# Projecting two pairs of neighbourhood heads early, and their place taken by half-size gate products

## The chip, the cores and the metric

The kernel runs on one core of a Trainium2 chip. Its time is the device time of one execution in microseconds (us); the median of three runs is 2477.17 us (2473.93 to 2483.84). The engines are named as the profile names them: PE is the matrix engine (TensorE), PEld its weight load, DVE the VectorE, ACT the ScalarE, POOL the GpSimd engine, SP the SyncE, which here only issues DMAs.

## The reference

One encoder block over 512 tokens of width 2048, in fp32:

```
mod    = silu(c) @ w_ada + b_ada          -> sh1, sc1, g1, sh2, sc2, g2
h      = rms_norm(x) * (1 + sc1) + sh1
[qa,ka,va, qb,kb,vb, ga,gb] = h @ w_in    # 8 + 2 + 2 heads A, 3 x 8 heads B, two gates of 2048
ya     = global attention (8 query heads, 2 key heads, qk-norm, rotary)
yb     = neighbourhood attention (8 heads, windows of 8 x 16 tokens, bias)
x      = x + g1 * ((sigmoid(ga) * (ya @ w_oa) + sigmoid(gb) * (yb @ w_ob)) @ w_out)
h2     = rms_norm(x) * (1 + sc2) + sh2
x      = x + g2 * ((silu(h2 @ w_gate) * (h2 @ w_up)) @ w_down)
out    = rms_norm(x)
```

## The kernel before, in words

**fp32 by parts.** Every fp32 operand of a product is held as a high part and a low part (`split`: ACT copies the high part, rounded, DVE subtracts it from the source to get the low part). A product is three matmuls, high x high, high x low, low x high (`mm3`, lines 187 to 189 of the kernel before). Weights are loaded by SP into `raw` tiles of 512 KB and split into `whl` tiles.

**Two forms of projection.** `form1` projects 256 output columns: 16 blocks of k, two column blocks, three matmuls that move 512 columns each. `group7` projects 512 output columns by a Strassen-like scheme of seven half-size products: four steps `s`, seven products, 84 matmuls a step that move 256 columns each, 336 in all, where two `form1` would need 192 matmuls of 512 columns. `wforms` makes the sums of weight blocks that the seven products need in tiles `ta` and `tb` on DVE, and splits them. At the end of a group, seven DVE additions gather the seven banks into a tile `c`.

**The order of the stages** around the change: global attention (`att_a`), with the `form1` of the gates A 12 to 15 beside it and those of the gates B 0 to 3 behind it; then five `group7` (three of gates B, `gates7`, and two of the values of the neighbourhood heads, `values7`, kept in DRAM as `v_d`); then the neighbourhood attention, four pairs of heads (`hp`), each pair with its own `form1` for queries and keys and then `att_b` for two heads; then the product with `w_oa` (its gates come back from DRAM as `g`), `w_ob`, `w_out`, and the feed-forward part, which is made of `group7` throughout. Gates are kept in DRAM as `sg_a`, `sg_b`. Queries and keys of the neighbourhood heads aren't kept; `form1` leaves them in PSUM banks `mm`, and `queries` and `tokens_split` split them from there into `qh`, `ql`, `kh`, `kl`.

**One neighbourhood head** (`att_b`) is a chain over engines: scores on PE into two banks `S` (12 matmuls of 256 columns), bias on DVE (`sb`, the bias tile `bm` comes by DMA on ACT's queue), maximum on DVE (`mx`), exponential on ACT (`e`), reciprocal and scaling on DVE, transposes on PE into bank `T`, a split into `pth` on ACT and `ptl` on DVE, and products with the values on PE into bank `Y`.

**The modulation beside it.** The second half of `mod` is computed as 96 accumulations on DVE before the feed-forward part (`acc`, line 379): each takes one 512 KB tile `mw` of w_ada that POOL's queue loads (line 357). They are handed out by `advance(mods)`: `slot` counts up by `pace["rate"]` at each unit of weights or half head and takes a step when the count reaches 1. 64 of the tiles run from the neighbourhood attention to the end of the product with `w_oa`, where `finish` takes what is left; 32 more run until the end of `w_out`.

**Memory.** Pools on one side of SBUF are a stack. `p_o` holds the tiles of the five `group7` (`c`, `ta`, `tb`, a few `raw` and `whl`). It is released behind them, and `p_w` (the modulation's tiles) and `p_b` (queries, keys, values, biases of `att_b`) are put in its place; the first write to each waits until every reader and writer of `p_o` has ended, the DMA of `c` into `v_d` too.

**Who sets the order.** A scheduler orders each engine's instructions when the kernel is built, from the program's order and priorities. Each engine then takes its own in that order and waits on semaphores; an instruction that waits holds all behind it on its engine.

Of the kernel before, what the change touches and what calls it, by code (L numbers as in the profile page):

```python
# [112 lines left out]
def encoder_block(ctx: ExitStack, tc, xp, xT, c, ada1_w, ada2_w, b_ada, norm1_w, w_in, q_norm_w, k_norm_w, bias,  # L113
# [11 lines left out]
    io = tc.alloc_tile_pool(name="io", bufs=3, side="right")  # L125
    aside = tc.alloc_tile_pool(name="aside", bufs=2, side="right")
# [220 lines left out]
    mod = {"pool": None, "queue": nc.gpsimd, "next": 0, "end": 0, "accs": 2, "loads": 3}  # L347
# [5 lines left out]
    def fetch():  # L353
        while mod["pool"] and len(fetched) < mod["loads"] and mod["next"] < mod["end"]:
            n = mod["next"] + {2: 32, 3: 32, 4: -32, 5: -32}.get(mod["next"] // KT, 0)
            w = mod["pool"].tile([P, 1024], F32, tag="mw", name="mw", bufs=mod["loads"])
# [10 lines left out]
    def ada_acc(bias, done):  # L367

        acc = mod["pool"].tile([P, 1024], F32, tag="acc", name="acc", bufs=mod["accs"])
# [18 lines left out]
    def row_sum(acc, q, tag, dst, then=None):  # L388
        few = mod["loads"] == 1
        hl = [io.tile([P, 512], F32R, tag="io", name="acc" + t) if few else  # L390
              mod["pool"].tile([P, 512], F32R, tag="acc" + t, name="acc" + t, bufs=1) for t in "hl"]
        split(*hl, acc[:, q * 512:(q + 1) * 512], pin=behind)
        soon.append((1 if few else 2, lambda: row_products(hl, tag, dst, then)))

    def row_products(hl, tag, dst, then):
        y = bank(tag)
# [10 lines left out]
        soon.append((1 if mod["loads"] == 1 else 2, keep))  # L407

    def ada_mod(k0, to):
# [9 lines left out]
        def done(acc):  # L419
            soon.append((1, functools.partial(row_sum, acc, 0, "Y", halves[0])))  # L420
            soon.append((4, functools.partial(row_sum, acc, 1, "Y", halves[1], lambda: soon.append((1, columns)))))
# [3 lines left out]
    def ada_gate(col, dst, tags):  # L425
        return ada_acc(col, lambda acc: soon.extend((1 + q * (4 if mod["loads"] == 1 else 1),
                                                     functools.partial(row_sum, acc, q, tags[q], dst[q])) for q in range(2)))
# [247 lines left out]

    def wforms(w, k0, c0, turned=False, late=False):
# [5 lines left out]
        ta = wq.tile([P, 1024], F32, tag="ta", name="ta", bufs=2)  # L682
# [49 lines left out]
    def group7(wsrc, xs, order, dst, first_group=False, by_tokens=False):  # L732
# [3 lines left out]
        for n, s in enumerate(order):  # L736
# [147 lines left out]

    for h in range(4):
# [3 lines left out]
    gates(sg_a, GA, 12, 16)  # L889
# [29 lines left out]
    def feature_forms(s):  # L919
# [3 lines left out]
        sa = p_o[0].tile([P, 1024], F32, tag="ta", name="sa", bufs=2)  # L923
# [18 lines left out]
    gates(sg_b, GB, 0, 4)  # L942
    wq = p_o[0]
    more_buffers(1, 1)
# [5 lines left out]
    def gates7(n):  # L950
# [7 lines left out]
        group7(lambda s: wforms(w_in, 4 * s, GB + n * 512), hs, range(4), dst)  # L958
        S.activation(c[0], c[0], AF.Sigmoid)
        for f in range(4):  # L960
            nc.scalar.dma_start(sg_b[4 * n + f].rearrange("p (t n) -> p t n", t=2), quarters(c[0])[:, f // 2, :, f % 2])

    def values7(hh):
        v = result().rearrange("p (i n) -> p i n", i=NT)
        d = [[v[:, 2 * t:2 * t + 2, f * 256:(f + 1) * 256] for f in range(2)] for t in range(2)]
        group7(lambda s: wforms(w_in, 4 * s, VB + hh * 512), hs, range(4), lambda: d, by_tokens=True)
        nc.scalar.dma_start(v_d[hh], v)

    for n in range(1, 4):
        gates7(n)  # L970
# [4 lines left out]
    more_buffers(0, 0)  # L975

    p_w = tc.alloc_tile_pool(name="p_w", bufs=1, side="right")
    mod.update(pool=p_w, end=64)
    g1_d, g2_d = ([dram.tile([1, 512], F32, name=f"g{n}d{q}") for q in range(4)] for n in (1, 2))
    columns_of = lambda ks: (ada_mod(k, (s2, b_sc2, n2, t2, b_sh2)) for k in ks)  # L980
    gate_of = lambda c, dst, tags="YT": (ada_gate(c * D + q * 512, dst[q:], tags) for q in (0, 2))
    mods.extend(columns_of((0, 4)))
    mods.extend(gate_of(2, g1_d))
    mods.extend(columns_of((8, 12)))
    for half_gate in gate_of(5, g2_d, "TT"):
        mods.extend((half_gate, iter([None] * 4)))
# [50 lines left out]

    def queries(hi, lo, b):
        tokens_split(hi[:, 64:], lo[:, 64:], b)
        for t in (hi, lo):  # L1040
            S.activation(t[:, :64], t[:, T:], AF.Copy)
# [24 lines left out]
    later.extend([lambda: None] * 4 + [lambda: pace.update(rate=0.68)])  # L1066
    for hp in range(4):
        hh, h0 = hp // 2, 2 * hp
        qs, ks = [pair(p_b, "q", T + 64, 3) for _ in range(2)], [pair(p_b, "k", T, 3) for _ in range(2)]
        form1([w_in], QB + h0 * HD, 2, hT, [[bank("mm"), bank("mm")]], lambda w, j, b: queries(*qs[j], b))  # L1070
        form1([w_in], KB + h0 * HD, 2, hT, [[bank("mm"), bank("mm")]], lambda w, j, b: tokens_split(*ks[j], b))
        if hp % 2 == 0:
            v = [pair(p_b, "v", 512, NT) for _ in range(NT)]
            for i in range(0, NT, 2):
                vr = raw_tile("vr")
                nc.sync.dma_start(vr.rearrange("p (i n) -> p i n", i=2), v_d[hh][:, i:i + 2])
                for e in range(2):
                    split(*v[i + e], vr[:, e * 512:(e + 1) * 512])
# [31 lines left out]

# [542 lines left out]
```

## Time and profile before

| | |
|---|---|
| profiled execution, its own time | 2471.66 us |
| span of the profile | 2469.5 us |
| median of three runs, lowest, highest | 2477.17, 2473.93, 2483.84 us |
| PE busy | 2434.0 us, 99% of the span |
| DVE busy | 2011.8 us, 81% |
| ACT busy | 1076.2 us, 44% |
| mean DMA rate | 187 GB/s |
| chain that ended last | PE 80%, DVE 11%, DMA 3%, issue 3% |

The busy time of PE is modelled, so 99% doesn't say that PE runs at its best; the number of matmuls in a stretch says more. Where matmuls of 512 columns stand without a gap, 233 start in 50 us; where those of 256 columns do, 450. "Idle before, releaser" of a row names what ended the engine's wait.

### The profile page before, as it was taken

What the parts mean: (1) busy time and instruction counts of PE and PEld (TensorE: products, weight loads), DVE (VectorE), ACT (ScalarE), POOL (GpSimd) and SP (SyncE); (2) the same over time, 40 slices, a digit from 0 to 9 for tenths busy, and PEclk for the clock granted to TensorE, in tenths of its full rate; (3) what the DMA queues carried; (4) which work ended last, traced back from release to release, by engine and by line L of the source; (5) the groups of instructions that cost most, each with busy time, mean ns of one, the idle gap of its engine ahead of it and who ended that gap; (6) DMA issues with size and microseconds to landing.
All of it is one profiled execution on the core that took longest, in us unless ns stands there. A gap on an engine that the chain in (4) does not pass through costs nothing.

```text
span 2469.5 us, 42360 instructions
## 1 busy us (share of the span) xinstructions
PE 2434.0 (99%) x17327; PEld 2279.5 (92%) x17327; DVE 2011.8 (81%) x2704; ACT 1076.2 (44%) x1470; POOL 152.1 (6%) x257
## 2 busy tenths in 40 slices
PE   8999999999999999999999999999999999999998
PEld 7888888999888888888999999999999998999997
DVE  8995778987587768667899899898898886787877
ACT  5223545544344533237744444444444454434333
POOL 0100000000012111021000000000000000000010
PEclk9999999999999999999999999999999999999999
DMA  9864232444578687966444354444444456546563
GB/s 355 314 238 154 85 100 78 148 129 145 201 250 273 233 305 247 309 211 215 139 160 160 131 171 153 130 152 142 159 153 154 131 187 222 197 151 234 192 248 123
DMA packets 213730, 461.77 MB, mean 187 GB/s; under 512 B 15152, under 2 KB 59552, under 8 KB 204832
## 3 DMA queue, kind: packets, MB, share of 16 engines
q1 hardware_dynamic: 173872, 308.71, 37.6%
q0 software_dynamic: 30160, 133.77, 15.4%
q10 hardware_dynamic: 9504, 16.58, 1.8%
q8 instruction: 136, 2.23, 0.4%
q14 instruction: 58, 0.48, 0.1%
HBM read 412.84 MB, written 46.17 MB: 186 GB/s over the span
## 4 chain that ended last, share of the span: by engine, by line
PE 80%; DVE 11%; DMA 3%; issue 3%; ACT 1%; POOL 0%; DVEq 0%; SPq 0%; POOLq 0%; ACTq 0%
PE mm L189 16%; PE mm L187 16%; PE mm L188 16%; PE S L187 6%; PE S L189 6%; PE S L188 6%; PE Y L187 3%; PE Y L188 3%; PE Y L189 3%; DVE raw L516 2%; DVE whl L169 2%; DMA mw<-in_ada_w 2%; DMA raw<-in_w_down 1%; PE T L189 1%; PE T L188 1%
## 5 line engine op out<-in xcount | busy, mean ns | idle before, releaser
L167 ACT ACTIVATE whl<-raw 128x1024 fp32r<-128x1024 f32 (+1 forms) x483 | 454.3, 943 | 659.4 <-PE mm L189 273.9
L169 DVE TENSOR_TENSOR whl<-raw,whl 128x1024 fp32r<-128x1024 f32 (+1 forms) x483 | 519.6, 1088 | 133.0 <-ACT whl L167 128.7
L167 ACT ACTIVATE whl<-ta 128x1024 fp32r<-128x1024 f32 x124 | 131.3, 1059 | 179.3 <-PE mm L189 110.2
L167 ACT ACTIVATE whl<-tb 128x1024 fp32r<-128x1024 f32 x124 | 131.4, 1059 | 172.4 <-PE S L189 119.8
L169 DVE TENSOR_TENSOR whl<-ta,whl 128x1024 fp32r<-128x1024 f32 x124 | 151.5, 1222 | 54.1 <-ACT whl L167 53.5
L379 DVE SCALAR_TENSOR_TENSOR acc<-mw,cact,acc 128x1024 f32<-128x1024 f32 x124 | 159.4, 1287 | 19.2 <-DMA mw<-in_ada_w 18.9
L169 DVE TENSOR_TENSOR whl<-tb,whl 128x1024 fp32r<-128x1024 f32 x124 | 151.1, 1219 | 7.8 <-ACT whl L167 7.3
L357 POOL DMA_DIRECT2D mw<-in_ada_w x115 | 61.5, 535 | 1381.1 <-DVE acc L379 836.1
L687 DVE TENSOR_TENSOR ta<-raw,ta 128x512 f32<-128x512 f32 x124 | 85.4, 689 | 53.8 <-DMA raw<-in_w_down 24.9
L686 DVE TENSOR_TENSOR ta<-raw 128x512 f32<-128x512 f32 x124 | 85.4, 689 | 29.5 <-DMA raw<-in_w_down 27.0
L187 PE MATMUL mm<-x56h,whl 128*128 128x256 f32 x336 | 92.5, 275 | 0.0
L188 PE MATMUL mm<-x56l,whl 128*128 128x256 f32 x336 | 92.4, 275 | 0.0
L189 PE MATMUL mm<-x56h,whl 128*128 128x256 f32 x336 | 92.4, 275 | 0.0
L187 PE MATMUL mm<-whl,s 128*128 128x256 f32 x320 | 88.1, 275 | 0.0
L187 PE MATMUL mm<-x3h,whl 128*128 128x256 f32 x320 | 88.0, 275 | 0.0
L188 PE MATMUL mm<-x3l,whl 128*128 128x256 f32 x320 | 88.0, 275 | 0.0
L189 PE MATMUL mm<-x3h,whl 128*128 128x256 f32 x320 | 88.0, 275 | 0.0
L187 PE MATMUL S<-x56h,whl 128*128 128x256 f32 x320 | 88.0, 275 | 0.0
L188 PE MATMUL S<-x56l,whl 128*128 128x256 f32 x320 | 88.0, 275 | 0.0
L189 PE MATMUL S<-x56h,whl 128*128 128x256 f32 x320 | 88.0, 275 | 0.0
L188 PE MATMUL mm<-whl,s 128*128 128x256 f32 x320 | 88.0, 275 | 0.0
L189 PE MATMUL mm<-whl,s 128*128 128x256 f32 x320 | 88.0, 275 | 0.0
(1879 smaller groups left out, 8916.8 us busy)
## 6 DMA issues: line engine op xcount, KB each, us to landing
raw<-in_w_in SPq DMA_DIRECT2D x133, 512.0 KB, 4.3
mw<-in_ada_w POOLq DMA_DIRECT2D x115, 512.0 KB, 4.5
raw<-in_w_gate SPq DMA_DIRECT2D x92, 512.0 KB, 4.5
raw<-in_w_up SPq DMA_DIRECT2D x88, 512.0 KB, 4.5
raw<-in_w_down SPq DMA_DIRECT2D x88, 512.0 KB, 5.0
raw<-in_ada_w POOLq DMA_DIRECT2D x29, 1024.0 KB, 7.3
raw<-in_w_out SPq DMA_DIRECT2D x48, 512.0 KB, 4.8
ffd<-c SPq DMA_DIRECT2D x10, 1024.0 KB, 4.8
```

Of the source, the lines that this page charges most:

```text
L167: high = pin(S.activation(hi, src, AF.Copy))
L169: latest[:] = [high, pin(eng.tensor_sub(lo, src, hi))]
L187: nc.tensor.matmul(o, lh, rh, start=start, stop=False, **kw)
L188: nc.tensor.matmul(o, lh, rl, start=False, stop=False, **kw)
L189: nc.tensor.matmul(o, ll, rh, start=False, stop=stop, **kw)
L357: mod["queue"].dma_start(w, ada2_w[n * P:(n + 1) * P, :])
L379: behind(V.scalar_tensor_tensor(acc, part, cact[:, k:k + 1], acc, op0=ALU.mult, op1=ALU.add))
L516: V.scalar_tensor_tensor(raw, raw, 1.0, call, op0=ALU.mult, op1=ALU.mult, accum_out=y)
L686: V.tensor_sub(t1, b12, b11)
L687: V.tensor_sub(t2_, b22, t1)
```

## The change

Three things move together.

1. In place of the `form1` of gates A 12 to 15 beside the global attention stands a projection of queries and keys of heads 0 and 1 of the neighbourhood attention (`project(0)`); in place of the `form1` of gates B 0 to 3 stands that of heads 4 and 5 (`project(2)`). Both are evacuated by ACT and kept in DRAM (`qk_d`). Later, pairs 0 and 2 load them (`kept`) and split them from SBUF; pairs 1 and 3 are projected as before (`fresh`).
2. The gates that lost their place are made by `group7`: seven groups in place of five.
3. The modulation starts earlier: 18 of its tiles come in the seven groups, three accumulations a group (`by_steps`), from a pool `p_w0` for the accumulator and one `mw` buffer in `p_o`; 30 more tiles in the neighbourhood attention, and 48 from `w_oa` on in a pool `p_w2` that is now opened ahead of `w_oa`. The `finish` behind `w_oa` is gone. To make room, `ta` has one buffer in the groups where it had two, and `raw` four where it had five.

```diff
 def slot():
     pace["due"] = min(pace["due"] + pace["rate"], 1.5)
+    if mod["then"] and not fetched and mod["next"] == mod["end"]:
+        mod.update(mod["then"].pop())
...
-    ta = wq.tile([P, 1024], F32, tag="ta", name="ta", bufs=2)
+    ta = wq.tile([P, 1024], F32, tag="ta", name="ta", bufs=ta_bufs[0])
...
+                if r == ORDER[2] and 0 < n <= by_steps:
+                    advance(mods)
...
+def project(hp):
+    for n, base in enumerate((QB, KB)):
+        def evac(w, j, b):
+            o = aside.tile([P, T], F32, tag="go", name="qo")
+            S.activation(o.rearrange("p (h e i) -> p h e i", e=2, i=P), apart(b), AF.Copy)
+            nc.scalar.dma_start(qk_d[hp // 2][n][:, j], o)
+        form1([w_in], base + 2 * hp * HD, 2, hT, [[bank("mm"), bank("mm")]], evac)
...
-gates(sg_a, GA, 12, 16)
+project(0)
...
-gates(sg_b, GB, 0, 4)
+project(2)
...
-more_buffers(1, 1)
+more_buffers(0, 1)
...
-for n in range(1, 4):
-    gates7(n)
+mod.update(mw=p_o[0], end=18, few=True, delays=(0, 3, 0))
+for base, to, n in [(GA, sg_a, 3)] + [(GB, sg_b, n) for n in range(4)]:
+    gates7(base, to, n, 1)
 for hh in range(2):
     values7(hh)
...
-mod.update(pool=p_w, end=64)
+mod.update(mw=p_w, sums=[(p_w, 1), (p_w0, 1)], end=48, loads=3, few=False, bank="mm", delays=(1, 6, 3))
...
+def kept(hp, qs, ks):
+    for n, ts in enumerate((qs, ks)):
+        r = raw_tile("qkr")
+        nc.sync.dma_start(r.rearrange("p (j t) -> p j t", j=2), qk_d[hp // 2][n])
+        for j, (hi, lo) in enumerate(ts):
+            o = 0 if n else 64
+            split(hi[:, o:], lo[:, o:], r[:, j * T:(j + 1) * T])
+            if not n:
+                wrap(hi, lo)
...
 for hp in range(4):
...
-    form1([w_in], QB + h0 * HD, 2, hT, ..., lambda w, j, b: queries(*qs[j], b))
-    form1([w_in], KB + h0 * HD, 2, hT, ..., lambda w, j, b: tokens_split(*ks[j], b))
+    (fresh if hp % 2 else kept)(hp, qs, ks)
...
+mod["then"].append(dict(mw=p_w2, sums=[(p_w2, 2)], end=96))
-pace["rate"] = 0.45
+pace["rate"] = 0.42
 for j in range(0, KT, 2):
     form1([w_oa], ...)
-finish()
```

How the built order moves, at three places. First, PE behind the last `group7`. Before (`Y` is the bank of its last product, `mm<-h0h` the first query projection):

```order
L189 MATMUL Y<-whl,h15l 128x256
L187 MATMUL mm<-h0h,whl 128x512
L188 MATMUL mm<-h0l,whl 128x512
L189 MATMUL mm<-h0h,whl 128x512
L187 MATMUL mm<-h0h,whl 128x512
```

After:

```order
L190 MATMUL Y<-whl,h15l 128x256
L188 MATMUL S<-kh,qh 128x256 x2
L189 MATMUL S<-kl,qh 128x256
L190 MATMUL S<-kh,ql 128x256
L188 MATMUL S<-kh,qh 128x256
L189 MATMUL S<-kl,qh 128x256
```

Before, 193 matmuls of two projections follow the last `Y`; after, the 12 score matmuls of head 0 do, then three of the projection of pair 1, then the scores of head 1, then 16 more of that projection ahead of the first transposes.

Second, ACT at the same place, after (`vd` is the DMA of the last `c` to DRAM, `qkr` the kept queries and keys, `vr` the kept values):

```order
L989 DMA vd_4028<-c 128x2048
L168 ACTIVATE qh<-qkr 128x512 x2
L1066 ACTIVATE qh<-qh 128x64 x2
L1066 ACTIVATE ql<-ql 128x64
L168 ACTIVATE kh<-qkr 128x512
L1066 ACTIVATE ql<-ql 128x64
L168 ACTIVATE kh<-qkr 128x512
L168 ACTIVATE vh<-vr 128x512 x4
L1019 DMA bm<-in_bias 128x512 x2
L168 ACTIVATE whl<-raw 128x1024 x3
L1019 DMA bm<-in_bias 128x512
L1039 ACT_TABLE_LOAD
```

Before, the issue of the two biases stood directly behind the first weight split after `vd`, far ahead of the first scores. After, ten pieces of splits stand between, all of which write tiles of `p_b`.

Third, DVE behind the fresh keys of the second pair (heads 2 and 3), after:

```order
L170 TENSOR_TENSOR kl<-mm,kh 128x512 x2
L170 TENSOR_TENSOR kl<-qkr,kh 128x512
L1033 SCALAR_TENSOR_TENSOR sb<-S,bm 128x512 x2
L1035 TENSOR_REDUCE mx_7772<-sb 128x2
L1035 TENSOR_REDUCE mx_7802<-sb 128x2
L1036 TENSOR_SCALAR mx_7772<-mx_7772 128x2
L170 TENSOR_TENSOR ql<-qkr,qh 128x512
L1036 TENSOR_SCALAR mx_7802<-mx_7802 128x2
L170 TENSOR_TENSOR kl<-qkr,kh 128x512
L1042 RECIPROCAL rs_7774<-sm_7773 128x2
L1033 SCALAR_TENSOR_TENSOR sb<-S,bm 128x512
L1044 TENSOR_SCALAR e<-e,rs_7774 128x256 x2
```

Before, the heads of a pair stood beside the whole projection of the next pair. After, four heads (2 to 5) follow each other here, since pair 2 has no projection of its own, and share 79 of the 192 matmuls of pair 3's projection. From the first of these rows to the last `ptl` split of head 5, DVE has 66 rows.

More of the change, by code (lines that the diff above doesn't have):

```diff
@@ L345, in encoder_block, with sum_tile @@
     t2 = const.tile([P, KT], F32, name="t2")
-    mod = {"pool": None, "queue": nc.gpsimd, "next": 0, "end": 0, "accs": 2, "loads": 3}
+    mod = {"mw": None, "loads": 1, "sums": [(p_w0, 1)], "few": False, "bank": None, "then": [], "delays": (1, 6, 3), "queue": nc.gpsimd, "next": 0, "end": 0}
+    def sum_tile():
+        pool, bufs = mod["sums"][0]
+        mod["sums"].append(mod["sums"].pop(0))
+        return pool.tile([P, 1024], F32, tag="acc", name="acc", bufs=bufs)
     fetched = collections.deque()
@@ L353, in fetch @@
     def fetch():
-        while mod["pool"] and len(fetched) < mod["loads"] and mod["next"] < mod["end"]:
+        while len(fetched) < mod["loads"] and mod["next"] < mod["end"]:
             n = mod["next"] + {2: 32, 3: 32, 4: -32, 5: -32}.get(mod["next"] // KT, 0)
-            w = mod["pool"].tile([P, 1024], F32, tag="mw", name="mw", bufs=mod["loads"])
+            w = mod["mw"].tile([P, 1024], F32, tag="mw", name="mw", bufs=mod["loads"])
             mod["queue"].dma_start(w, ada2_w[n * P:(n + 1) * P, :])
@@ L367, in ada_acc @@
     def ada_acc(bias, done):
-        acc = mod["pool"].tile([P, 1024], F32, tag="acc", name="acc", bufs=mod["accs"])
+        acc = sum_tile()
         if bias is not None:
@@ L405, in keep, with ada_mod @@
                 then()
-        soon.append((1 if mod["loads"] == 1 else 2, keep))
-    def ada_mod(k0, to):
+        soon.append((2 if mod["delays"][2] > 1 else 1, keep))
+    def ada_mod(k0, to, tag):
         halves = [dram.tile([1, 512], F32, name=f"md{k0}{q}") for q in range(2)]
@@ L883, in att_a @@
         keep_y(h, yb)
+    qk_d = [[dram.tile([P, 2, T], F32, name=f"qk{hp}{n}") for n in range(2)] for hp in (0, 2)]
+    def project(hp):
[5 more added lines that the diff above has]
+            form1([w_in], base + 2 * hp * HD, 2, hT, [[bank("mm"), bank("mm")]], evac)
     for h in range(4):
@@ L975, in encoder_block @@
     more_buffers(0, 0)
+    ta_bufs[0] = 2
     p_w = tc.alloc_tile_pool(name="p_w", bufs=1, side="right")
[L978 to L986 removed]
+    mod.update(mw=p_w, sums=[(p_w, 1), (p_w0, 1)], end=48, loads=3, few=False, bank="mm", delays=(1, 6, 3))
     fetch()
@@ L1064, in attended, with kept_values, fresh @@
         split(*hl, yr)
-    later.extend([lambda: None] * 4 + [lambda: pace.update(rate=0.68)])
+    pace["rate"] = 0.65
+    def kept(hp, qs, ks):
[6 more added lines that the diff above has]
+                if not n:
+                    wrap(hi, lo)
+    def kept_values(hh):
+        v = [pair(p_b, "v", 512, NT) for _ in range(NT)]
+        for i in range(0, NT, 2):
+            vr = raw_tile("vr")
+            nc.sync.dma_start(vr.rearrange("p (i n) -> p i n", i=2), v_d[hh][:, i:i + 2])
+            for e in range(2):
+                split(*v[i + e], vr[:, e * 512:(e + 1) * 512])
+        return v
+    def fresh(hp, qs, ks):
+        form1([w_in], QB + 2 * hp * HD, 2, hT, [[bank("mm"), bank("mm")]], lambda w, j, b: queries(*qs[j], b))
+        form1([w_in], KB + 2 * hp * HD, 2, hT, [[bank("mm"), bank("mm")]], lambda w, j, b: tokens_split(*ks[j], b))
     for hp in range(4):
@@ L1069, in encoder_block @@
         qs, ks = [pair(p_b, "q", T + 64, 3) for _ in range(2)], [pair(p_b, "k", T, 3) for _ in range(2)]
-        form1([w_in], QB + h0 * HD, 2, hT, [[bank("mm"), bank("mm")]], lambda w, j, b: queries(*qs[j], b))
-        form1([w_in], KB + h0 * HD, 2, hT, [[bank("mm"), bank("mm")]], lambda w, j, b: tokens_split(*ks[j], b))
+        (fresh if hp % 2 else kept)(hp, qs, ks)
         if hp % 2 == 0:
[L1073 to L1078, printed above, removed]
+            v = kept_values(hh)
         if hp == 3:
@@ L1298, in first_pairs @@
         early[1] = ff_pair(0, 1, [c_p.tile([P, 1024], F32R, tag=t, name="e1", bufs=1) for t in ("mw", "acc")], nc.sync)
-    mod.update(pool=c_p, queue=nc.gpsimd, end=128, accs=1, loads=1)
+    mod.update(mw=c_p, sums=[(c_p, 1)], queue=nc.gpsimd, end=128, loads=1, few=True, delays=(1, 5, 1))
     for n in range(FU):
```

53 lines of the change are left out of this document (33 added, 20 removed).

## The prediction

> **What bounds the kernel now.** I read the page's busy times first, then the table of stretches, then the rows around the places that the change touches.
>
> ```profile
> span 2469.5 us, 42360 instructions
> PE 2434.0 (99%) x17327; PEld 2279.5 (92%) x17327; DVE 2011.8 (81%) x2704; ACT 1076.2 (44%) x1470; POOL 152.1 (6%) x257
> PE 80%; DVE 11%; DMA 3%; issue 3%; ACT 1%; POOL 0%; DVEq 0%; SPq 0%; POOLq 0%; ACTq 0%
> ```
>
> PE bounds the kernel, so a matmul saved counts where PE is dense, and a wait of PE counts everywhere. The stretches (us, then busy time and count of PE, PEld, DVE, ACT, POOL, the granted clock, the DMA share, GB/s) show where it is dense:
>
> ```profile
> 484.90:522.20 37.30, 37.30 (x337) 37.30 (x336) 31.15 (x40) 17.35 (x18) 0.00 (x0) 1.00 0.45 141
> 500.00:550.00 50.00, 50.00 (x450) 50.00 (x450) 40.69 (x50) 23.21 (x25) 0.00 (x0) 1.00 0.43 134
> 700.00:760.00 60.00, 59.59 (x303) 51.25 (x302) 48.84 (x68) 25.45 (x51) 11.30 (x21) 1.00 0.78 260
> 760.00:820.00 60.00, 59.67 (x301) 50.66 (x300) 46.06 (x65) 22.68 (x45) 12.24 (x22) 1.00 0.83 278
> 820.00:880.00 60.00, 53.28 (x254) 44.70 (x253) 47.55 (x72) 36.09 (x60) 9.41 (x16) 0.94 0.71 251
> 950.00:1000.00 50.00, 50.00 (x233) 43.79 (x232) 45.02 (x56) 17.38 (x22) 7.95 (x15) 1.00 0.81 278
> ```
>
> One `group7` takes 37.3 us, with 336 matmuls and DVE busy for 31. A matmul of 256 columns costs 50/450 = 0.111 us, one of 512 columns 50/233 = 0.2146. The neighbourhood attention (640 to 820) is dense too; PE loses 6.7 us, and some clock, only from 820 to 880, where heads 6 and 7 stand beside `w_oa`.
>
> **Part 1: the products.** The two `form1` beside the global attention and the two behind it stay in number: gates become queries and keys. Two more groups add 672 matmuls of 256 columns, 74.7 us; pairs 0 and 2 drop 384 of 512 columns, 82.4 us. On PE: **-7.7 us**. Dropped too are 16 weight splits, and 6 of 17 loads of ACT's function table; both lie beside PE, and I cost them at nothing. The new stores (eight of 256 KB on ACT's queue) replace eight stores of gates; the gates' new stores go out from `c` as those of the other groups do.
>
> **Part 2: the place behind the last group.** There the cover of PE is gone. Before:
>
> ```profile
> 626.78 0.28 PE L189 MATMUL Y<-whl,h15l 128*128 128x256 f32 x1
> 626.89 0.38 PE L187 MATMUL mm<-h0h,whl 128*128 128x512 f32 x1
> 628.99 0.69 DVE L773 TENSOR_TENSOR c<-c,Y 128x512 f32<-128x512 f32 x1
> 629.72 0.33 ACTq L967 DMA_DIRECT2D vd<-c  x1
> 633.90 0.82 ACTq L993 DMA_DIRECT2D bm<-in_bias  x2
> ...
> raw<-in_w_in SPq DMA_DIRECT2D x133, 512.0 KB, 4.3
> bm<-in_bias ACTq DMA_DIRECT2D x8, 256.0 KB, 3.7
> ```
>
> The first five rows are of the timeline (start, duration), the last two of the DMA issues (size, median us to landing). The last product of the groups ends at about E = 626.9, and PE goes on at once. The bias is the first write to `p_b`: it goes out 4.2 us after the store of `c`, when that has read its tile. All this was hidden by 41 us of projections. After, queries and keys wait for the same release and PE has nothing else: the scores stand first in its order, and the weights of pair 1 can't be there early, since the four `raw` buffers hold `qkr` and `vr`, which can't be split before `p_b` is free. The durations:
>
> ```profile
> L1007 DVE SCALAR_TENSOR_TENSOR sb<-S,bm 128x512 f32<-128x512 f32 x15 | 10.0, 682 | 1.1 <-PE S L189 1.1
> L1009 DVE TENSOR_REDUCE mx<-sb 128x2 f32<-128x512 f32 x15 | 9.9, 674 | 0.0
> L169 DVE TENSOR_TENSOR whl<-raw,whl 128x1024 fp32r<-128x1024 f32 x31 | 37.7, 1219 | 18.6 <-ACT whl L167 18.6
> L169 DVE TENSOR_TENSOR kl<-mm,kh 128x512 fp32r<-128x512 f32 x8 | 5.3, 690 | 6.4 <-ACT kh L167 6.4
> L167 ACT ACTIVATE qh<-mm 128x512 fp32r<-128x512 f32 x8 | 4.7, 587 | 8.0 <-PE mm L189 8.0
> L1041 ACT ACTIVATE ql<-ql 128x64 fp32r<-128x64 f32 x8 | 2.0, 253 | 8.6 <-DVE ql L169 8.6
> L167 ACT ACTIVATE vh<-vr 128x512 fp32r<-128x512 f32 x8 | 4.7, 622 | 6.0 <-DMA vr<-vd 6.0
> ```
>
> Back to back, each starts about 0.08 us before the recorded end of the last. From E: `c` complete +1.1 (in the after order no weight split stands between the seven additions, three stood there before), store read +5.3. ACT: two `qh`, two wraps, a wrap of `ql`, the first `kh` end at +7.3, and the first `kl` on DVE at +8.0: the scores of head 0 run from +8.0 to +9.3. The other splits keep ACT until about +10.1, and only then are the biases issued; they land 3.7 us later, +13.8. Two `sb` and two maxima (4 x 0.6) end at +16.2, then comes the first weight split, 1.2: PE gets its first projection matmul at +17.5. Idle: 17.5 less 1.3 of scores, 16.2 us. From then on 58 matmuls of 0.2146 and the heads' own cover DVE. The clock adds to it:
>
> ```profile
> 821.92 0.49 PE L187 MATMUL S<-kh,qh 128*128 128x256 f32 x2 [1.02 <-ACT kh L167]
> 823.31 0.38 PE L188 MATMUL S<-kl,qh 128*128 128x256 f32 x1 [0.89 <-DVE kl L169]
> 826.81 0.63 PE L188 MATMUL mm<-ya0l,whl 128*128 128x512 f32 x1
> 827.24 0.63 PE L189 MATMUL mm<-ya0h,whl 128*128 128x512 f32 x1
> 828.15 0.38 PE L187 MATMUL mm<-ya0h,whl 128*128 128x512 f32 x1
> ```
>
> After idle pieces of 1.0 and 0.9 us, matmuls of 512 columns start 0.43 us apart until 827.7: half speed for some 3.4 us, a loss of 1.7. So **+17.9 us**. Bounds: with the bias landing in 2.5 us and one step less of waiting, 14; with slower landings beside three loads of `mw`, 20.
>
> **Part 3: heads 2 to 5 in a row.** DVE from the keys of head 3 to the last split of head 5 has, for four heads, 8 each of `sb`, maximum, two small ones, two scalings, `ptl`; beside them 5 weight splits, 5 accumulations, 10 half splits (keys, queries, values, a sum). The rows not shown yet:
>
> ```profile
> L379 DVE SCALAR_TENSOR_TENSOR acc<-mw,cact,acc 128x1024 f32<-128x1024 f32 x42 | 53.8, 1281 | 14.8 <-DMA mw<-in_ada_w 14.5
> L169 DVE TENSOR_TENSOR ptl<-T,pth 128x512 fp32r<-128x512 f32 x12 | 8.3, 689 | 3.3 <-ACT pth L167 2.8
> L1018 DVE TENSOR_SCALAR e<-e,rs 128x256 f32<-128x256 f32 x26 | 7.9, 346 | 0.1
> L1010 DVE TENSOR_SCALAR mx<-mx 128x2 f32<-128x2 f32 x14 | 2.3, 161 | 0.0
> ```
>
> Less 0.08 each: 8 x (0.60 + 0.59 + 2 x 0.08 + 2 x 0.27 + 0.61) = 20.0; 5 x 1.14 + 5 x 1.20 + 10 x 0.61 = 17.8; together 37.8 us. PE has there 96 matmuls of 256 columns (10.7), 32 transposes (some 3, an estimate from 0.4 us for four) and 79 of the projection (17.0): 30.6. DVE bounds the stretch: with 0.8 ahead (the first `kh`) and 0.9 behind (the last products with the values) 39.5 us, +8.9. DVE also waits at its start for scores and exponentials; I take **+10**, between +6 (the chains overlap better) and +15 (DVE waits at each head). Before, 301 and 303 matmuls in 60 us show that these heads cost PE next to nothing.
>
> **Part 4: the modulation.** The groups get three accumulations each, 3 x 1.2, on DVE's 31 of 37.3 us: covered. At their start DVE was late before (first row, of the waits: us in all, times, longest):
>
> ```profile
> PE mm L189 <- DVE whl L169: 1.9, 2, 1.3
> ...
> 873.03 0.49 PE L398 MATMUL T<-acch,ones_r 128*128 128x512 f32 x1 [2.20 <-ACT acch L167]
> 875.29 0.59 PE L398 MATMUL T<-accl,ones_r 128*128 128x512 f32 x1 [1.76 <-DVE accl L169]
> 864.23 6.63 DMA yr<-y
> ```
>
> One accumulation and single `ta` there: **+1** (0 to 5). The stall at 873, 4 us and a half-speed phase of 1.7, came from the row sum behind an attention output that landed after 6.6 us, amid loads of `mw` (the last row, of the chain). After, 18 tiles are gone to the groups, and `w_oa` takes them at rate 0.42 without `finish`: I take **-5** of this 5.7 (0 to -10 with the smaller gaps from 840 on).
>
> **The sum:** -7.7 + 17.9 + 10 + 1 - 5 = +16.2, from the profiled execution's 2471.66 to **2488 us**. That execution lies 0.2% under the median, within the runs' spread.
>
> [...]
>
> **Rivals.**
> - *No change.* The relief of the DMA queues is full (-10), parts 2 and 3 take their low ends (14 and 6), part 4 none: -7.7 + 14 + 6 - 10 = +2.3, 2474 us. For it: 14.5 us of DVE's waits for `mw` in the rows above. Against: PE lost little of that.
> - *Faster*, by one mechanism: the projections of pairs 1 and 3 go on covering, so that parts 2 and 3 cost nothing: -7.7 + 1 - 5 = -11.7, 2460 us. The change is faster at all where parts 2 and 3 together stay under 11.7. Against: even if the release came with the last DVE addition (+1.1) and the biases were issued ahead of the splits, they would land at +4.8, `sb`, maxima and the weight split would end at +8.5, and part 2 would still cost 7; the order has the splits first, and DVE's 37.8 us of part 3 stand whatever PE does.
> [...]
> - *The groups become DVE's.* With one `ta` and four `raw`, if each of seven groups loses 2 us: +14, 2502 us. Against: 3.6 us more leave DVE under 35 of 37.3.
>
> **Chances.** The forecast (2480 to 2497) 0.55; no change 0.25; groups 0.09; half speed 0.06; faster 0.05. The range leaves out the half speed and the faster case: 2474 to 2503. 0.5% of the median, 12.4 us, is about what a measurement here can tell from none; the forecast, with its middle at +16.2, passes it in some 7 of 10 cases, 0.38, the groups and the half speed do, 0.15, and the faster case does so in most. So slower 0.53, same 0.43, faster 0.04.
>
> **What would show it.** Right: a gap of about 16 us on PE behind the last `Y` product, its scores released by `kl`, then its first `mm` by `whl` on DVE, and the first `sb` by the DMA of `bm`; PE at some 75% for 40 us behind the keys of head 3; seven groups of 37.3 us; no wait at the row sums beside `w_oa`. Wrong: groups over 38 us, a gap under 12 us, or a stretch of four heads as dense as before.

## The result, and the profile after

| | before | after |
|---|---|---|
| median of 6 runs | 2477.66 us | 2491.04 us |
| range | 2473.16 to 2483.84 | 2488.00 to 2495.78 |
| profiled execution (span) | 2471.66 (2469.5) | 2491.34 (2489.6) |

The change makes the kernel slower: after divided by before is 1.0053, with a 95% interval of 1.0039 to 1.0067. That is +13 us in the medians and +20 in the two spans; the profiled execution before lies 6 us under the median of its six. Below, a time against the kernel before is given as a ratio with its interval, against runs of the kernel before on the same chip.

The page of the kernel after: PE's busy time is almost as before though it has less to do, its row of slices has a 7 and its clock's row an 8 in the twelfth slice, from 685 to 747 us, and the chain of work that ended last runs less over PE (80% before) and more over DVE (11%):

```profile
span 2489.6 us, 43083 instructions
PE 2432.4 (98%) x17615; PEld 2289.0 (92%) x17615; DVE 2050.2 (82%) x2766; ACT 1085.3 (44%) x1484; POOL 150.8 (6%) x255
PE   7999999999979999999999999999999999999998
PEclk9999999999989999999999999999999999999999
PE 64%; DVE 18%; issue 9%; DMA 6%; ACT 1%; POOL 0%; DVEq 0%; POOLq 0%; ACTq 0%
```

The slices lead to the place behind the last group. Its timeline (start, duration, what ended the idle time ahead), by PE, ACT with its queue, and DVE:

```profile
706.88 0.28 PE L190 MATMUL Y<-whl,h15l 128*128 128x256 f32 x1
714.98 0.80 PE L188 MATMUL S<-kh,qh 128*128 128x256 f32 x2 [7.83 <-ACT kh L168]
723.77 0.80 PE L188 MATMUL mm<-h0h,whl 128*128 128x512 f32 x1 [5.57 <-ACT whl L168]
...
712.76 1.15 ACT L168 ACTIVATE qh<-qkr 128x512 fp32r<-128x512 f32 x2 [13.02 <-DMA vd<-c]
714.77 0.39 ACTq L1019 DMA_DIRECT2D bm<-in_bias  x1
715.50 2.18 ACT L168 ACTIVATE vh<-vr 128x512 fp32r<-128x512 f32 x4
722.66 1.06 ACT L168 ACTIVATE whl<-raw 128x1024 fp32r<-128x1024 f32 x1 [4.98 <-DMA raw<-in_w_in]
...
708.08 0.69 DVE L785 TENSOR_TENSOR c<-c,Y 128x512 f32<-128x512 f32 x1
721.34 1.29 DVE L1033 SCALAR_TENSOR_TENSOR sb<-S,bm 128x512 f32<-128x512 f32 x2 [2.61 <-DMA bm<-in_bias]
723.79 1.22 DVE L170 TENSOR_TENSOR whl<-raw,whl 128x1024 fp32r<-128x1024 f32 x1
```

PE's last product of the groups ends at about E = 707.0, which answers to 626.9 before, where the next product followed at once. Now PE has one burst of scores at 715.0 and then nothing until pair 1's first projection at 723.8, E + 16.8. The row that releases it is ACT's split of a weight, and that waited for the weight's DMA.

The table of stretches (us, busy time and count of PE, PEld, DVE, ACT, POOL, clock, DMA share, GB/s) shows a steady group, the gap with its clock, and heads 2 to 5 with theirs:

```profile
521.60:558.90 37.30, 37.30 (x337) 37.30 (x336) 34.02 (x43) 17.34 (x18) 1.58 (x3) 1.00 0.58 184
709.70:726.70 17.00, 6.16 (x22) 5.37 (x23) 10.32 (x17) 8.38 (x16) 3.04 (x5) 0.50 0.84 307
773.50:816.40 42.90, 37.87 (x207) 31.56 (x208) 39.34 (x77) 26.50 (x63) 2.75 (x5) 0.92 0.67 212
781.35:788.10 6.75, 6.25 (x25) 5.55 (x25) 6.55 (x14) 3.94 (x8) 1.07 (x2) 0.50 0.65 213
```

A group takes 37.3 us as before, with DVE busy for 34.0 instead of 31. Heads 2 to 5 run from the first score of head 2 at 773.5 to the last product of head 5 at 816.4. These are DVE's first row there and its last split of head 5:

```profile
773.51 1.34 DVE L170 TENSOR_TENSOR kl<-mm,kh 128x512 fp32r<-128x512 f32 x2 [7.16 <-ACT kh L168]
...
814.63 0.69 DVE L170 TENSOR_TENSOR ptl<-T,pth 128x512 fp32r<-128x512 f32 x1 [1.44 <-ACT pth L168]
```

From the one to the end of the other DVE has 76 rows (not the 66 given with the built order), busy for 38.3 of 41.8 us.

Beside `w_oa` the wait at the row sum has changed its cause. It was 2.2 and 1.8 us for the split of the sum, and now PE waits for the copy `ada_o` of an earlier one, which stands on DVE behind a product with a late gate:

```profile
886.38 0.69 DVE L1154 TENSOR_TENSOR oa<-g,mm 128x512 f32<-128x512 f32 x1 [3.39 <-ACT g L1153]
886.99 0.67 DVE L410 COPY ada_o<-Y 1x512 f32<-1x512 f32 x1
...
887.80 0.47 PE L406 MATMUL Y<-acch,ones_r 128*128 128x512 f32 x1 [1.97 <-DVE ada_o L410]
```

To compare kernels I use one number, PE's *excess* from 700 to 900 us: for each of PE's rows the distance to the start of the next, less the steady 0.2146 or 0.111 us of 512 or 256 columns, or 0.057 for 128, which is an estimate, about half of 0.111 (in both traces most transposes start 0.109 apart, and with that the 19.7 and 42.2 below would be 17.2 and 38.9), summed over the rows whose next one starts in the window. It holds idle time and half speed alike. Before it is 19.7, after 42.2. Over the whole span it is 83 and 111. The span less the excess is, by its making, the number of products times their steady steps, so that its fall of 7.7 us repeats the count of part 1 and doesn't measure it. The window doesn't hold the same work in every kernel; taken from the last product of the groups to the last of `w_oa`, the excess is 22 before and 42 after.

### The profile page after: what moved, and what is told of

Its sections match the earlier page's. It is cut to its first block, busy times and chain, and to the rows that moved or that the text cites. A ratio compares the mean times of both kernels' runs of the same rounds, so it can differ in the third digit from the quotient of the medians.

```text
span 2489.6 us, 43083 instructions
## 1 busy us (share of the span) xinstructions
PE 2432.4 (98%) x17615; PEld 2289.0 (92%) x17615; DVE 2050.2 (82%) x2766; ACT 1085.3 (44%) x1484; POOL 150.8 (6%) x255
## 3 DMA queue, kind: packets, MB, share of 16 engines
q0 software_dynamic: 29872, 132.73, 15.6%
## 4 chain that ended last, share of the span: by engine, by line
PE 64%; DVE 18%; issue 9%; DMA 6%; ACT 1%; POOL 0%; DVEq 0%; POOLq 0%; ACTq 0%
PE mm L188 12%; PE mm L190 12%; PE mm L189 12%; PE S L190 5%; PE S L188 5%; PE S L189 5%; DVE whl L170 5%; PE Y L188 2%; PE Y L189 2%; PE Y L190 2%; DVE raw L524 2%; DMA mw<-in_ada_w 2%; DMA raw<-in_w_up 2%; DVE acc L388 1%; DMA raw<-in_w_down 1%
## 5 line engine op out<-in xcount | busy, mean ns | idle before, releaser
L170 DVE TENSOR_TENSOR whl<-raw,whl 128x1024 fp32r<-128x1024 f32 (+1 forms) x483 | 512.8, 1076 | 103.1 <-ACT whl L168 98.9
L168 ACT ACTIVATE whl<-ta 128x1024 fp32r<-128x1024 f32 x132 | 139.8, 1059 | 196.7 <-PE mm L190 107.4
L168 ACT ACTIVATE whl<-tb 128x1024 fp32r<-128x1024 f32 x132 | 139.8, 1059 | 181.6 <-PE S L190 118.1
L170 DVE TENSOR_TENSOR whl<-ta,whl 128x1024 fp32r<-128x1024 f32 x132 | 161.1, 1221 | 51.0 <-ACT whl L168 50.9
L170 DVE TENSOR_TENSOR whl<-tb,whl 128x1024 fp32r<-128x1024 f32 x132 | 160.9, 1219 | 6.6 <-ACT whl L168 6.3
L697 DVE TENSOR_TENSOR ta<-raw,ta 128x512 f32<-128x512 f32 x132 | 90.8, 688 | 64.1 <-DMA raw<-in_w_down 25.1
L696 DVE TENSOR_TENSOR ta<-raw 128x512 f32<-128x512 f32 x132 | 90.9, 689 | 30.3 <-DMA raw<-in_w_down 27.7
L698 DVE TENSOR_TENSOR tb<-raw 128x512 f32<-128x512 f32 x132 | 90.4, 685 | 1.6 <-DMA raw<-in_w_down 0.4
```

Of the source, the lines that this page charges most:

```text
L168: high = pin(S.activation(hi, src, AF.Copy))
L170: latest[:] = [high, pin(eng.tensor_sub(lo, src, hi))]
L696: V.tensor_sub(t1, b12, b11)
L697: V.tensor_sub(t2_, b22, t1)
L698: V.tensor_sub(t3, b22, b12)
```

## The experiments

All are edits of the kernel after, timed five times each in the first six runs and 11 or 12 times in the others.

| experiment | ratio to before (95%) | excess, 700 to 900 us |
|---|---|---|
| the kernel after | 1.0053 (1.0039 to 1.0067) | 42.2 |
| biases issued early | 1.0073 (1.0060 to 1.0085) | 41.0 |
| values aside | 1.0068 (1.0055 to 1.0081) | 41.2 |
| odd pairs saved | 1.0070 (1.0056 to 1.0084) | 44.7 |
| no sums in heads 2 to 5 | 1.0071 (1.0058 to 1.0083) | 43.5 |
| stage without sums | 1.0042 (1.0029 to 1.0054) | 36.2 |
| sums without loads | 1.0045 (1.0033 to 1.0058) | 38.0 |
| modulation alone | 0.9988 (0.9979 to 0.9997) | 17.4 |
| pair 2 alone saved | 0.9997 (0.9985 to 1.0010) | 21.1 |
| pair 2 behind the groups | 1.0006 (0.9996 to 1.0016) | 23.6 |
| pair 1 alone saved | 1.0013 (1.0002 to 1.0024) | 26.3 |
| modulation alone, values aside | 0.9987 (0.9976 to 0.9997) | 15.6 |
| values aside, no sums | 0.9980 (0.9968 to 0.9991) | 22.5 |

### Biases issued early

```diff
+    load_bias(0)
+    load_bias(1)
     for hp in range(4):
```

> The changed kernel, but the biases of heads 0 and 1 are issued on ACT's queue before anything of pair 0 is loaded, instead of behind the splits of its queries. In the changed kernel's trace the last product behind the seventh group starts at 706.9, the first score comes at 714.98, the first bias addition at 721.3 and the first projection of pair 1 at 723.8. Theory W (weights): the first projection ends the gap, and it waits for its own weights, because saved queries, keys and values hold the four raw buffers into which the weights are to be loaded; the bias lies beside it. Then the first bias addition comes up to 5 us earlier, the first projection at the same place within 1 us, and the time is that of the changed kernel, 2488 to 2492. Theory B (biases, as the prediction's part 2 had it: scores, bias, then the DVE half of the weights): the gap shrinks by what the bias comes earlier, 3 to 5 us, and the time is 2485 to 2488.

Measured: 2492.28 us. In its timeline the last product starts at 704.4, and

```profile
710.30 0.82 ACTq L1020 DMA_DIRECT2D bm<-in_bias  x2
...
717.05 1.28 DVE L1040 SCALAR_TENSOR_TENSOR sb<-S,bm 128x512 f32<-128x512 f32 x2
720.72 1.06 ACT L168 ACTIVATE whl<-raw 128x1024 fp32r<-128x1024 f32 x1 [4.63 <-DMA raw<-in_w_in]
721.83 0.80 PE L188 MATMUL mm<-h0h,whl 128*128 128x512 f32 x1 [5.21 <-ACT whl L168]
```

The first `sb` no longer waits for its bias, it comes 12.5 us behind the last product's end instead of 14.3, and the first projection stands at 17.3 where it stood at 16.8. So the weights end this gap and the biases lie beside it: theory W, 0.3 us above its range.

### Values aside

```diff
-            vr = raw_tile("vr")
-            nc.sync.dma_start(vr.rearrange("p (i n) -> p i n", i=2), v_d[hh][:, i:i + 2])
             for e in range(2):
-                split(*v[i + e], vr[:, e * 512:(e + 1) * 512])
+                vr = aside.tile([P, T], F32, tag=("y", "go")[i // 2], name="vr")
+                nc.sync.dma_start(vr, v_d[hh][:, i + e])
+                split(*v[i + e], vr)
```

> The changed kernel, but the saved values are loaded in 512-wide pieces into the four small tiles that also carry heads' outputs, so that two of the four raw buffers are free for pair 1's weights while the seventh group still runs. With that the order puts 60-odd projections of pair 1 straight behind the last group's products, and heads 0 to 3 later among them. Theory W: the weights are there, PE goes on without a gap (13.9 us idle and about 3.5 us of half clock gone); what is given back is that heads 0 and 1 have less beside them, 0 to 8 us. Time 2473 to 2484. Theory B (pool memory of p_b, splits and biases of pair 0 set the gap whatever the weights do): queries, keys and values are split on the same engines ahead of the weights, and the time stays within 3 us of the changed kernel, 2488 to 2494.

Measured: 2491.55 us. The gap closes: PE goes from the last product to pair 1's first projection in one step.

```profile
703.66 0.28 PE L190 MATMUL Y<-whl,h15l 128*128 128x256 f32 x1
703.77 0.38 PE L188 MATMUL mm<-h0h,whl 128*128 128x512 f32 x1
```

So theory W is right on what held the gap open. But the time is that of the kernel after, and the expected 2473 to 2484 was missed, since nearly all came back among the heads. PE's waits from there on (us in all, times, longest), and what stood on DVE at one of them:

```profile
PE S L189 <- DVE kl L170: 9.3, 2, 5.0
PE Y L188 <- ACT vh L168: 3.5, 1, 3.5
PE S L188 <- DMA raw<-in_w_in: 2.6, 1, 2.6
```

```profile
761.54 1.28 DVE L388 SCALAR_TENSOR_TENSOR acc<-mw,cact,acc 128x1024 f32<-128x1024 f32 x1 [0.17 <-DMA mw<-in_ada_w]
763.04 1.28 DVE L388 SCALAR_TENSOR_TENSOR acc<-mw,cact,acc 128x1024 f32<-128x1024 f32 x1 [0.21 <-DMA mw<-in_ada_w]
764.24 1.28 DVE L170 TENSOR_TENSOR kl<-mm,kh 128x512 fp32r<-128x512 f32 x2
...
764.98 0.58 PE L189 MATMUL S<-kl,qh 128*128 128x256 f32 x1 [4.27 <-DVE kl L170]
```

The score wants the low part of the keys. Its high part begins on ACT at 759.14, but DVE makes the low part only at 764.24, behind three sums of the modulation (two are shown) and a weight split that stand ahead in its order; the sums had waited for their loads, by 1.24, 0.17 and 0.21 us. In these rows DVE kept to that order, with 4.27 us of PE's idle time as the price.

### Odd pairs saved

```diff
-    project(0)
+    project(1)
...
-    project(2)
+    project(3)
...
-        (fresh if hp % 2 else kept)(hp, qs, ks)
+        (kept if hp % 2 else fresh)(hp, qs, ks)
```

> The changed kernel, but pairs 1 and 3 are projected ahead and saved, and pairs 0 and 2 are projected at their place. So pair 0's projection stands behind the seventh group as in the kernel before, heads 0 to 3 have pair 2's projection beside them, and heads 4 to 7 have the product with w_oa. Place theory (part 2 of the prediction): the whole gap of about 17 us goes. Heads theory: with four heads beside one projection the stretch that cost +8 to +10 in the changed kernel still costs that, so 2472 to 2478; if what made that stretch slow was only that pair 2's saved tiles were split in the middle of it, it goes too and the time is 2462 to 2468. Rival: heads 4 to 7 in front of w_oa have too little beside them and the gap only moves there; then 2482 to 2490.

Measured: 2492.95 us: the rival's mechanism, 3 us above its range. The gap at the groups is gone here too (the excess from 700 to 750 us is 0.3), and the waits stand between 750 and 754 and, above all, from 810 to 860, with heads 4 to 7 in front of `w_oa`:

```profile
PE S L188 <- DVE sb L1033: 5.4, 3, 3.6
PE S L188 <- ACT kh L168: 4.3, 2, 2.4
PE mm L188 <- ACT ya2h L168: 3.8, 1, 3.8
```

Two ways to fill the gap, and neither wins anything. What the first expectations had in common, that a gap closed is a gap won, is wrong.

### No sums in heads 2 to 5

```diff
+        pace["rate"] = 0.0 if hp in (1, 2) else 0.65
         for j in range(2):
             att_b(...)
+        pace["rate"] = 0.65
```

> The changed kernel, but the modulation makes no partial sums in heads 2 to 5 (five steps fewer there, in the trace 4 sums of 1.28 us and one split of 0.68, 5.8 us of DVE), and makes them up in the projection of pair 3 and after it. DVE theory (part 3 of the prediction: 37.8 us of DVE work against 30.6 of PE in that stretch): the stretch shortens by 4 to 6 us and the time is 2484 to 2488. Chain theory: the stretch is as long as the chain score, bias, exponential, transpose, split of one head behind the other with nothing to fill it, DVE has gaps enough, and the time stays at 2489 to 2493, more if the sums then disturb w_oa.

Measured: 2492.24 us, so the chain theory's time. The wait in that stretch is the same 2.25 us, for the same release, as in the kernel after (at 780.02 there):

```profile
780.25 0.35 PE L188 MATMUL S<-kh,qh 128*128 128x256 f32 x1 [2.25 <-DVE sb L1033]
```

But the run hardly tests the DVE theory. The sums were only put off, from 707 to 890 us there are still 31 of 36, and pair 3's projection, which hands them out again, runs beside these very heads: four sums stand between the keys of head 3 and the last split of head 5, where the kernel after has five. DVE is busy there for 35.8 us instead of 38.3, and the four heads take 41.4 us instead of 42.8.

### Stage without sums, and sums without loads

```diff
+    left_out = {n for n in range(18, 62) if n % KT != KT - 1}
...
         for k in range(KT):
+            if base + k in left_out:
+                continue
...
-    pace["rate"] = 0.65
+    pace["rate"] = 0.1
...
-    pace["rate"] = 0.42
+    pace["rate"] = 0.1
```

```diff
+            if 20 < mod["next"] < 62 and mod["next"] != 48:
+                w = last_w[0]
+            else:
+                w = mod["mw"].tile(...)
```

> The changed kernel, but 42 of the 44 loads of modulation weights and the sums made of them that fall between the last group and the end of the product with w_oa are left out (so the modulation is not the reference's). In four variants before this one the excess of PE's rows over their steady step between 700 and 900 us was 41 to 45 us, against 20 in the kernel before, wherever the saved pairs stood. Theory S (the sums: DVE takes its work in order, the sums are 42 x 1.28 = 54 us of it and waited 11.6 us for their loads, and heads' steps stand behind them): the excess falls by 13 to 22 us and the time is 2470 to 2478. Theory O (the order of PE's row and the length of one head's chain make the waits, with DVE under 80% busy): within 4 us of the changed kernel, 2487 to 2493.

> The changed kernel, but in the same stage the sums of the modulation are made of a tile that is already there instead of one loaded anew: 40 loads of 512 KB, 21 MB of the 50 MB that the stage moves, are gone, and the sums stay (the modulation is not the reference's). It splits theory S: if DVE's time for the sums is what costs, the time stays at 2487 to 2493; if it is the wait for their loads, or other loads (weights, saved queries, keys and values, biases) that land late beside them, 2472 to 2484, and the DMAs of saved tiles land in 3 to 4 us where they took 4.4 to 6.9. Theory O: 2487 to 2493.

Measured: 2485.94 and 2487.07 us, by the ratios 2 to 8 us less than the kernel after and the variants so far (their intervals overlap that of the kernel after). The first is neither theory's number, the second lies at the lower edge of 2487 to 2493. In the first, 4 sums are left of 36 between 707 and 890 us, and the gap behind the groups stands as it was:

```profile
713.53 0.80 PE L188 MATMUL S<-kh,qh 128*128 128x256 f32 x2 [7.83 <-ACT kh L168]
722.37 0.80 PE L188 MATMUL mm<-h0h,whl 128*128 128x512 f32 x1 [5.61 <-ACT whl L168]
```

What delays the weights in the gap these two don't tell: of the loads of the modulation that go out there, three in the kernel after, the second run has the same three (at 713.28) and the first still two. The first projection waits 5.61 and 5.73 us, with all the loads 5.57. Most of what is won lies in heads 2 to 5 and at `w_oa`. The windows of the four heads, the first run's and then the second's, test the DVE theory that the run before this one left open:

```profile
772.30:809.50 37.20, 33.59 (x198) 28.65 (x199) 33.86 (x73) 25.60 (x62) 0.49 (x1) 0.95 0.55 177
774.50:816.20 41.70, 36.94 (x208) 30.31 (x208) 39.26 (x77) 26.37 (x64) 0.00 (x0) 0.96 0.50 160
```

With one sum left there instead of five the heads take 37.1 us instead of 42.8, 5.7 less (PE's own steady steps in them are only 1.9 us fewer); with the sums but without their loads they take 41.6. So here it is DVE's time for the sums that costs, not the loads, and the chain of one head, which is the same in all three, doesn't set the length alone.

### The modulation alone, and one saved pair

The first keeps the gates and all four projections where they were, the second saves pair 2 and leaves the gates of group A's last blocks beside the global attention (the edit shown is the second's; the first also has `gates(sg_b, GB, 0, 4)` for `project(2)`, and all pairs `fresh`):

```diff
-    project(0)
+    gates(sg_a, GA, 12, 16)
...
-        (fresh if hp % 2 else kept)(hp, qs, ks)
+        (kept if hp == 2 else fresh)(hp, qs, ks)
```

> The kernel before with part 4 alone: the modulation's first 15 sums go beside the five groups, the rest is spread over the products behind; gates, queries and keys are projected where the kernel before has them. Part 4 by the prediction: +1 at the groups' starts (in the changed kernel's trace +2), -5 at the product with w_oa: 2471 to 2475, 1 to 5 us faster than before. Rival: the wait at the row sums only turns into one on the gate's load and the copy of the sum, as in the changed kernel's trace (1.97 us at 887.8), and nothing is won, 2475 to 2479.

> Half of the change: only pair 2 is projected ahead and saved, pairs 0, 1 and 3 are projected at their place, six groups instead of seven, and the modulation begins in the groups as in the changed kernel. Place theory (part 2): pair 0 covers the place behind the last group, so the 17 us there go; part 1 gives half, -3.8; heads 4 and 5 alone have less beside them. Time 2472 to 2480. Cover theory (each saved pair takes 41 us of products away from the heads, and the heads give some 11 us of that back as waits wherever it was taken): the result lies half way between the modulation alone and the changed kernel, 2479 to 2484.

Measured: 2473.2 us, ratio 0.9988, 3.0 us faster than before with an interval of 0.7 to 5.2: part 4 by itself pays, and no row sum is among PE's waits at `w_oa` any more. With one saved pair: 2476.68 us, as before, inside what the place theory gave and below the cover theory's 2479 to 2484. The second saved pair, which is pair 0 and brings the gap, costs the rest, though not by the gap alone: with the odd pairs saved there is no gap, and the time is no shorter. Its heads 4 and 5 still pay, with the same 2.25 us behind `sb`; from 760 to 810 us the excess is 11.1.

### Pair 2 behind the groups

```diff
-    project(2)
+    gates(sg_b, GB, 0, 4)
...
     pace["rate"] = 0.65
+    project(2)
```

> Both pairs are projected ahead and saved, as in the changed kernel, and the heads' loop is the changed kernel's, but pair 2 is projected behind the last group instead of ahead of the first; the first four blocks of group B's gates go back to its place, so there are six groups. Place theory: pair 0's saved queries and keys are fetched and split while pair 2's products run, so the 17 us behind the last group go, part 1 gives half of its 7.7, and the time is that of the kernel with pair 2 alone saved, 2473 to 2480. Conservation theory (two variants of the changed kernel closed that gap and were no faster: two saved pairs leave the heads some 22 us short of products wherever the products go): pair 2's products are over before the heads begin, so the heads are as short as before, 2485 to 2492.

Measured: 2474.84 us, ratio 1.0006: place theory. Both pairs are saved and fetched, the loop of the heads is the kernel's after, and some 12 us are gone (1.0006 against 1.0053, with half of part 1's gain given up). PE goes on at once:

```profile
665.81 0.28 PE L190 MATMUL Y<-whl,h15l 128*128 128x256 f32 x1
665.92 0.38 PE L188 MATMUL mm<-h0h,whl 128*128 128x512 f32 x1
```

What tells it from the two variants that closed the gap in vain is the number of projections behind the last group: three here and with one saved pair, two there. So this run does two things at once: it closes the gap, and it gives the stage a third projection.

### Pair 1 alone, and the modulation with values aside

> As the kernel with pair 2 alone saved, but it is pair 1: heads 0 to 3 stand in a row beside pair 2's projection, heads 4 and 5 beside pair 3's. If one saved pair costs the heads the same wherever it stands: within 3 us of the kernel with pair 2 alone, 2474 to 2480. If the stretch of heads 2 to 5 is dear because DVE has sums to make in it and here heads 0 to 3 stand where its queue is emptier: 2470 to 2474.

> The modulation alone, and the saved values loaded in 512-wide pieces into the small tiles, which leaves the four raw buffers to the weights in the heads' stage. If weights that come late behind values cost anything in that stage (a wait of 2.4 us at 702.6 us among the first projections of the kernel with the modulation alone), 2469 to 2472; if not, as the modulation alone, 2472 to 2476.

Measured: 2478.5 us, ratio 1.0013, not told apart from pair 2 alone (0.9997, the intervals overlap). In its trace heads 0 to 3 take 36.9 us, where heads 2 to 5 take 42.1 with pair 2 alone, but from the last group to the end of `w_oa` the excess is 27 against 22: what the heads win is lost behind them. The second: 2471.71 us, within the 2469 to 2472 of the first case, but against the kernel before on the same chip its ratio is 0.9987, as that of the modulation alone. The weights that come earlier win nothing there, and the wait at 702.6 stays, at 705.7 there, 2.99 us for the low part of a query. These two kernels with the modulation alone are the fastest here that compute everything, 3 us under the kernel before.

### Values aside, no sums

Both edits together: the one that closed the gap and the one that empties DVE's queue.

> The changed kernel with the values loaded into the small tiles, so that pair 1's weights come early, and with the 42 loads and sums of the modulation left out between the last group and the end of the product with w_oa (the modulation is not the reference's). With the values aside alone the gap behind the last group closed, but scores then waited 9.3 us for low parts of keys (kl), which stood on DVE behind sums that waited for their loads. Theory Q (DVE's queue: what was won at the gap was lost to the sums ahead of the heads' own steps): without sums these waits go, and the time falls by 12 to 20 us against the values aside alone, to 2472 to 2480; leaving the sums out without the values aside gave only 5, since there the gap stood. Theory F (two projections are too little to fill the heads' chains, with DVE free or not): as with the sums left out alone, 2483 to 2488.

Measured: 2469.72 us, ratio 0.9980 (0.9968 to 0.9991). Against the values aside alone, 1.0068, that is 22 us; the same sums left out with the gap open gave 3 to 8. Theory Q, by 2 us more than its range. Of 9.3 us of waits for `kl` 0.2 are left:

```profile
PE S L188 <- DVE sb L1045: 3.3, 1, 3.3
PE S L188 <- DMA raw<-in_w_in: 2.4, 1, 2.4
...
PE S L189 <- DVE kl L170: 0.2, 1, 0.2
```

The windows from 660 to 900 us of the two, values aside first, show PE and the clock gain what DVE lost:

```profile
660.00:900.00 240.00, 218.24 (x1254) 192.53 (x1253) 188.49 (x279) 109.48 (x207) 31.13 (x55) 0.96 0.70 234
```

```profile
660.00:900.00 240.00, 230.61 (x1341) 202.65 (x1341) 158.56 (x262) 117.03 (x218) 14.86 (x25) 0.99 0.54 178
```

It is no better kernel, since it leaves work out. It shows that two things hold this stage, and that taking either away alone shows little. Two things it doesn't show: how much the kernel before, or the modulation alone, would gain without these sums, so that the 22 us aren't the price of the two saved pairs; and whether it is DVE's time for the sums or their wait for loads that counts outside heads 2 to 5, since both are gone.

## Why the prediction was right, point by point

**Part 1, -7.7.** No run times this term alone. What it is made of holds: a steady group takes 37.30 us after as before, and the counts of products are those of the prediction.

**Part 2, +17.9: the size right, the way to it in part wrong.** In the trace the excess from 710 to 730 is 17.0 us. From the kernel after to pair 2 behind the groups the ratio falls by 0.0047, 12 us (1.0068 to 1.0073 in the variants that kept the cost gives 15 to 17); with half of part 1 given up in that kernel, 3.9, that is 16 to 20, for the place and the third projection together. The first score came at E + 8.0, as forecast (released by `kh` on ACT, not by `kl`). Behind it two steps failed and cancelled, which is luck. The prediction had the biases issued behind all splits at E + 10.1 and the DVE half of the weights behind `sb` as the last link, at E + 17.5. They were issued at E + 7.8, while the splits of the values ahead of them in ACT's order were still to run, and landed after 6.5 us instead of 3.7; and the last link, at E + 16.8, was the landing of the weights themselves, then ACT's half. The idle time was 13.9 us, not 16.2. The half speed was dearer, about 3.1 us and not 1.7: the clock stayed at 0.50 for 17 us, through scores and first projections.

**Part 3, +10: the mechanism right, the size some 2 to 4 too large.** The list of DVE's work was exact: 76 rows of the kinds that it names, busy for 38.3 us against 37.8. DVE does bound the stretch, 38.3 of the 41.8 us between its first and last row there; without four of the five sums the heads take 5.7 us less. The four heads took 42.8 us, where the sum had 39.5. PE's steady steps in them come to 29.4, which leaves an excess of 13.5. The term mis-sized is the one for the kernel before: "these heads cost PE next to nothing", but by the same count heads 2 to 5 have an excess of 5.8 there. The difference is +8. By the times, with pair 2 alone saved against the modulation alone, the ratio rises by 0.0009, 2 us, with half of part 1 won: about +6, with an uncertainty of some 4. PE's steady steps fill 69% of the stretch, not 75%. What was missed is that DVE's order costs PE at other places of the stage too, as with the values aside (9.3 us for `kl`) or, with pair 1 alone, behind the four heads (8.3 us for `ql`, `whl` and `kl`).

**Part 4, -4.** Measured alone: -3.0 (-5.2 to -0.7). The start of the groups cost about 2 instead of 1. "No wait at the row sums beside `w_oa`" was wrong for the kernel after, where a late gate took the stall's place, and right for the modulation alone.

**The sum and the rivals.** The terms measured give -7.7 + 17 + 7 - 3 = +13, and the medians differ by 13.4. That they agree so closely is luck, since two of the terms are uncertain by 2 to 4 us. The two traces differ by 20: the excess rises by 16 up to head 2 and by 8 in heads 2 to 5, falls by 4 from there to the end of `w_oa`, and rises by 7 outside this stage, which no run follows up. The forecast of 2488 also gains from its base: it added 16.2, some 3 us too much, to a profiled execution 6 us under the median. The rival *faster* needed parts 2 and 3 to cost under 11.7 together; they cost some 24. Pair 1's weights did come late, as part 2 has it; with the values aside they were early, and the time still didn't fall. Only without the sums of the stage as well is it 2469.7, 5 us under the kernel before. *Half speed*, the 0.06 of the chances, means part 3 at half the clock throughout; the clock stood at 0.50 there for 6.75 us, from 781.35 to 788.10, and at 0.92 in the mean of the stretch. *Groups* stayed at 37.3.

**What the prediction did not see** is that parts 2 and 3 are not two prices to be added or saved one by one. Filling the gap by bringing a projection forward takes it from the heads, and they then show DVE's queue. With three projections behind the groups, 41 or 42 sums between 660 and 890 us stand beside a time that is within 0.2% of before; with two and the gap closed, there are 39, and leaving out all but 7 takes 22 us off.

What stays open: whether sums moved out of the stage, into `w_ob` and the products behind, would keep these 22 us in a kernel that computes everything. It wasn't tried.

## What to carry to other kernels

Products that move to a cheaper place leave behind the latencies they covered; count how many of them stand beside the heads (or whatever has a long chain on other engines), not only what each costs. When a gap is closed and the time doesn't move, look at what the waits became, and take away two suspects together before acquitting either: here the gap alone gave nothing, the sums alone 3 to 8 us, and the sums with the gap closed 22. Buffers that hold loads not yet usable (here saved tensors in the weights' buffers) push the next loads behind them, so give them a place of their own (here that closed the gap, but by itself won no time).

## What the runs showed of the hardware

- After idle time the clock fell 2.7 us behind the last product (E = 707.0, 0.50 from 709.7 on), and 3 us of dense scores at 715.0 did not bring it back; it came at 726.7, 3 us into the projections. Between 640 and 910 us it stood at 0.50 four times in the traces of the kernels before and after: for 3.4 us from 824.35 and from 875.55 before, for 17.1 us from 709.64 and for 6.8 us from 781.32 after. In the 3.4 us ahead of these PE was idle for 1.9, 2.7, 2.5 and 2.1 us; in the last 3.4 us of the 17.1 it was idle for 0.5, and in those of the other three not at all.
- ACT's queue issued DMAs while ACT's own earlier activations still ran: the biases went out at 714.77, during the split of a key (0.61 us from 714.31), though four splits of values stand ahead of them in ACT's order, which ran from 715.50 for 2.2 us. So these issues left ahead of rows that stand before them in the order.
- The biases' landing took 6.5 us behind the groups where the median was 3.7, at a DMA share of 0.84, and the weights issued from 714.75 on took 7.7 us in the median where they took 4.3 before. Six loads of weights, three of the modulation and the biases go out there within 14 us. Which of them delays the others is open: no run takes all three loads of the modulation away there.
